# A decoder step on one core: 48 expert blocks multiplied in plain float32 instead of in split parts

## The chip, the core and the metric

The kernel runs on one core of a Trainium2 chip. The metric is the device time of one launch in microseconds. Times of the kernel before are from three runs; the trace is of one further execution, taken by the hardware profiler. The engines are TensorE (PE, and PEld for its weight loads), VectorE (DVE), ScalarE (ACT), GpSimd (POOL) and SyncE (SP, which here only issues transfers).

## What is computed

One inference step of a one-layer decoder over 512 prompt tokens and 64 sample tokens: a modulation by a condition vector, one combined projection, retention and dilated attention, an output projection and a layer norm, and then a layer of 16,384 experts with one row each in two tables:

```python
def block(xb):
    q = (xb @ w_q).reshape(PEER_BLOCK, H_PEER, 2, DK_PEER // 2)
    s = jnp.einsum('thsc,hskc->thsk', q, sub_keys).astype(jnp.float32)
    sv, si = lax.top_k(s, TOPK_PEER)
    cand = (sv[:, :, 0, :, None] + sv[:, :, 1, None, :]).reshape(PEER_BLOCK, H_PEER, TOPK_PEER * TOPK_PEER)
    cv, ci = lax.top_k(cand, TOPK_PEER)
    i0 = jnp.take_along_axis(si[:, :, 0], ci // TOPK_PEER, axis=-1)
    i1 = jnp.take_along_axis(si[:, :, 1], ci % TOPK_PEER, axis=-1)
    e = i0 * N_KEYS + i1
    g = jax.nn.softmax(cv, axis=-1)
    a = jax.nn.gelu(jnp.einsum('td,thkd->thk', xb, u_tab[e]), approximate=False)
    return jnp.einsum('thk,thkd->td', (g * a).astype(xb.dtype), v_tab[e])
```

D_MODEL is 1024, N_KEYS 128, H_PEER 8 and TOPK_PEER 16, so each token picks 128 experts. Everything is float32.

## The kernel before

The expert layer of the first 384 prompt tokens (three tiles of 128; ND = 384) is computed densely. The 16,384 experts are 128 blocks of 128. For block i the kernel multiplies the block's rows of u by the tokens' h2 (the input of the expert layer, transposed), takes the Gelu, multiplies by the block's gates and then by the block's rows of v, and adds up over the blocks in six PSUM banks. The remaining 128 prompt tokens and the 64 sample tokens take their experts by gathered rows: POOL issues the gathers (L1111), DVE multiplies (L1120, L1129), a few at each call of `advance`, which ties them to a point of the program by a copy of one element on POOL (`pace`, L1143).

A float32 product is made in **split parts**: `split` makes of x a rounded high part (ACT copy to the type fp32r) and the rest as a low part (a subtraction, to fp32r), and `mm3` (L423 to L425) does three matmuls, high by high, high by low and low by high. h2 lies split in the tiles `h2h` and `h2l`.

The program's order around the change:

- The w_q projection, the scores (L1458) and the selection of the 16 best (`top16`, DVE) for four tiles of tokens.
- `u_ahead(HEAD)`, with HEAD = 16: the u part of the first 16 of 48 blocks whose activations are computed ahead (those with i % 8 < 3). `u_part` loads the block (L1421, SP, 512 KB) into `wraw`, splits it (L1424 on ACT, L1425 on POOL), does 24 matmuls of 128x384 into a PSUM tile `tr` and the Gelu (L1430, ACT). `u_ahead` stores the result in DRAM (`actD`, L1439).
- `spread(t)` for three tiles: `route` (DVE, with one exponential on ACT, L1030) finds experts and gates; the **spread** then makes the gate of every token and expert. For four tokens at a time (a q; 32 q a tile, 96 in all) it builds one-hots: `oh1` on DVE (L1487), `oh0` one of four on ACT (L1493, L1494), one of four on POOL in every other q and the rest on DVE (L1496). Four plain float32 matmuls of 128x128 (L1497) multiply them, ACT copies the result to `stage` (L1498), and after eight q SP stores 2 MB in DRAM (L1502). After every fourth q one more ahead block is issued (`u_ahead(AHEAD)`), 24 in all.
- `u_ahead(128)` issues the last eight of the 48.
- The main loop over 128 blocks: gates are loaded for eight blocks at a time (L1578; 12 pieces, one for each store of the spread), the activation is loaded (L1589) or computed by `u_part`, and `v_part` loads v (L1558), splits it, multiplies activation and gates (`wt`, L1562) and does 18 matmuls of 128x512 for the block.

Instructions of one engine run in the order in which the scheduler laid them down, by a model of its own, when the program was built; engines wait for each other only where data or a buffer asks for it. The `wraw` tiles go round in 3 buffers (RB), the split parts in 4 (UB), the PSUM tiles `tr` in 2, the one-hots in 3.

Of the kernel before, what the change touches and what calls it, by code (L numbers as in the profile page):

```python
# [8 lines left out]
F32 = mybir.dt.float32  # L9
# [4 lines left out]
AF = mybir.ActivationFunctionType  # L14
OP = mybir.AluOpType
# [42 lines left out]
CU = 1  # L58
# [166 lines left out]
def body(tc, I, O, dbg=None):  # L225
    nc = tc.nc
    PE, DVE, ACT, POOL, SP = nc.tensor, nc.vector, nc.scalar, nc.gpsimd, nc.sync
# [6 lines left out]
    def fv(ap):  # L234
        return ap.bitcast(F32)

    def pool(name, side=None, space=None):
        kw = {"reuse_waits": "tile"} if space is None else {"space": space}
        if side:
            kw["side"] = side  # L240
        return tc.alloc_tile_pool(name=name, bufs=1, **kw)
# [17 lines left out]
    def tr_ps():  # L259
        return psum("tr", 2)  # L260
# [4 lines left out]
    def const(name, pl=P0, eng=SP):  # L265
        a = I[name]
        t = pl.tile(list(a.shape), F32, name="k" + name, tag="k" + name)
        eng.dma_start(t, a)
        return t
# [25 lines left out]
    def copy_old(n, ins):  # L295
        with tc.issue_after(ins):
            for _ in range(n):
                p = next(old, None)
                if p:
                    SP.dma_start(*p)  # L300
# [4 lines left out]
    def w_raw(pl=W, bufs=RB):  # L305
        return pl.tile([128, 1024], F32, name="wraw", tag="wraw", bufs=bufs)
# [126 lines left out]
    E = pool("halves", side="right")  # L433
# [21 lines left out]
    POOL.memset(cst, 0.0)  # L455
    SP.dma_start(cst[:, :, 0:9], I["cT"])
    ident = const("c_ident", eng=ACT)
    sel19 = const("c_sel", eng=ACT)
    iota = const("c_iota", eng=ACT)
    ACT.activation(cst[:, :, 0:9], cst[:, :, 0:9], AF.Silu)  # L460
    scT = A.tile([128, 8, 65], F32, name="scT")
# [56 lines left out]
    for g in range(NG):  # L518
        for o in range(VEC_G[g], VEC_G[g + 1], 512):
            e = min(o + 512, VEC_G[g + 1])  # L520
            ps = ac_ps()
# [529 lines left out]
    for c in range(2):  # L1051
        s = S1.tile([128, 4, 128], F32, name="scs", tag="scs", bufs=1)
        for z2 in range(2):
# [8 lines left out]
            ps = ac_ps()  # L1062
# [138 lines left out]
    for g in range(NG):  # L1201
# [8 lines left out]
        for hf in range(2):  # L1210
# [30 lines left out]
            for pp in range(2):  # L1241
# [38 lines left out]
                for c in range(4):  # L1280
                    for i, (vt, x, b) in enumerate(src[c]):
                        for h2, rows, hd, _ in heads:
                            PE.matmul(po[rows, 128 * c:128 * c + 128], v[vt][:, 64 * hd:64 * hd + 64], pts[h2][x][:, 128 * b:128 * b + 128],
                                      start=i == 0, stop=i == len(src[c]) - 1)
# [63 lines left out]
    ND = 128 * TD  # L1348
# [33 lines left out]
    h2h, h2l = [slot("x4"), slot("x5")], [slot("x6"), slot("x7")]  # L1382
    h2p = pair(h2h, h2l)
    ws = {}
    for c, ts in ((0, (0, 1, 2, 3)), (1, (0, 1, 2, 3)), (2, (0,)), (3, (0,)), (2, (1,)), (3, (1,)), (2, (2, 3)), (3, (2, 3))):
# [4 lines left out]
        for t in ts:  # L1390
            z = zs[t]
            ps = proj_n(w, mix, tiles[t])
# [23 lines left out]
    actD = {i: DR.tile([128, ND], F32, name=f"act{i}") for i in ahead}  # L1416
    ACTP = pool("act")

    def u_part(i):
        u = w_raw().rearrange("p (k e) -> p k e", e=128)  # L1420
        SP.dma_start(u, I["uT"][i])  # L1421
        uh = w_hi().rearrange("p (k e) -> p k e", e=128)
        ul = w_lo().rearrange("p (k e) -> p k e", e=128)
        ACT.activation(uh, u, AF.Copy)  # L1424
        POOL.tensor_tensor(ul, u, fv(uh), op=OP.subtract)  # L1425
        ps = tr_ps()
        for k in range(8):
            mm3(ps[:, 0:ND], (uh[:, k, :], ul[:, k, :]), h2p(k, slice(0, ND)), k == 0, k == 7)
        a = ACTP.tile([128, ND], F32, name="act", tag="act", bufs=4)
        ACT.activation(a, ps[:, 0:ND], AF.Gelu)  # L1430
        return a

    pre = iter(ahead)

    def u_ahead(n):
        for _ in range(n):
            i = next(pre, None)
            if i is not None:
                copy_old(CU, SP.dma_start(actD[i], u_part(i)).ins)  # L1439

    C = pool("route", side="right")
    sv = [C.tile([128, 16, 16], F32, name=f"sv{t}") for t in range(NT)]
    si = [C.tile([128, 16, 16], U32, name=f"si{t}") for t in range(NT)]
    C1 = pool("scores", side="right")
    for c in range(4):
        keys = C1.tile([128, 4, 128], F32, name="keys", tag="keys", bufs=2)
        SP.dma_start(keys, I["keysT"][:, 4 * c:4 * c + 4, :])
# [7 lines left out]
        for t in range(NT):  # L1455
            ps = ac_ps()
# [125 lines left out]
    for i in range(128):  # L1582
# [4 lines left out]
        if i in actD:  # L1587
            a = ACTP.tile([128, ND], F32, name="act", tag="act", bufs=4)
            SP.dma_start(a, actD[i])  # L1589
        else:  # L1590
            a = u_part(i)
# [41 lines left out]
```

## Time and profile before

| | us |
|---|---|
| three runs: median (lowest to highest) | 2486.14 (2481.27 to 2489.11) |
| the profiled execution: time, span | 2492.82, 2490.8 |
| busy in the span: PE, DVE, POOL, ACT | 2239.6, 1781.7, 1191.4, 1006.7 |

The mean granted clock of PE is 0.943 of full speed. All times within the profile count from the start of the span; the rows below are shown as the profile has them. A line such as "L1425 POOL TENSOR_TENSOR wlo<-wraw,whi 128x1024" names the line of the program, the engine, the operation and the tiles written and read. "Idle before" is the time in which that engine did nothing just before, with what released it. A float32 matmul is recorded as two pairs of a weight load and a pass. Matmuls overlap, so a single one's duration is longer than the step from one start to the next.

### The profile page before, as it was taken

The page shows a single profiled execution, that of the slowest core. Times are in us where ns is not written, and L with a number is a line of the kernel's source. Part 1 is how long each engine was busy: PE and PEld are TensorE (multiplying, and loading weights), DVE is VectorE, ACT ScalarE, POOL GpSimd, SP SyncE. Part 2 cuts the span into 40 slices and gives each one's busy share as a digit, 9 for nine tenths or more (in the row PEclk, how much of TensorE's full clock was granted, in tenths as well). Part 3 has the DMA queues.
Part 4 walks back from the last instruction along what each step waited for, and adds up shares of the span by engine and source line. Part 5 has one row for each costly group of instructions (what it writes and reads, how often), then busy time and mean ns, then how long its engine had stood idle before and what let it go on. Part 6 is the DMA issues. An engine that isn't in the chain of part 4 may idle for free.

```text
span 2490.8 us, 35646 instructions
## 1 busy us (share of the span) xinstructions
PE 2239.6 (90%) x12729; PEld 1894.2 (76%) x12729; DVE 1781.7 (72%) x3069; ACT 1006.7 (40%) x1661; POOL 1191.4 (48%) x942
## 2 busy tenths in 40 slices
PE   7889999958799996889888898799999999999995
PEld 4775566646777874889778888688888888888884
DVE  3463122255678778779999995888788888888875
ACT  2462222234455462233357786333333333333342
POOL 1021011043025645323566564877677777777742
PEclk7899999988899997899989999999999999999998
DMA  8786886566798997386767678799899999999951
GB/s 295 251 294 205 285 289 200 168 196 212 243 331 279 332 360 255 116 285 223 275 210 257 238 249 290 250 328 352 320 328 333 331 315 337 330 331 338 335 166 51
DMA packets 222494, 671.38 MB, mean 270 GB/s; under 512 B 27307, under 2 KB 80299, under 8 KB 218827
## 3 DMA queue, kind: packets, MB, share of 16 engines
q1 hardware_dynamic: 162016, 448.32, 52.6%
q0 software_dynamic: 59904, 220.62, 24.7%
q8 instruction: 100, 1.64, 0.3%
q14 instruction: 78, 0.64, 0.1%
q10 hardware_dynamic: 396, 0.16, 0.0%
HBM read 614.38 MB, written 112.40 MB: 292 GB/s over the span
## 4 chain that ended last, share of the span: by engine, by line
PE 51%; DVE 22%; DMA 12%; issue 6%; POOL 4%; ACT 3%; SPq 1%; POOLq 0%; DVEq 0%; ACTq 0%
PE mm L423 7%; PE mm L424 7%; PE mm L425 7%; PE tr L425 3%; PE tr L424 3%; PE tr L423 3%; DVE wlo L316 3%; PE ac L748 3%; DVE oh L1496 3%; DVE ys L1129 2%; PE ac L423 2%; PE ac L425 2%; PE ac L424 2%; DMA row<-in_u_dram,e 2%; POOL row L1111 1%
## 5 line engine op out<-in xcount | busy, mean ns | idle before, releaser
L316 DVE TENSOR_TENSOR wlo<-wraw,whi 128x1024 fp32r<-128x1024 f32 x304 | 415.3, 1370 | 266.7 <-ACT whi L315 243.0
L315 ACT ACTIVATE whi<-wraw 128x1024 fp32r<-128x1024 f32 x304 | 319.6, 1057 | 444.3 <-PE mm L424 171.5
L1425 POOL TENSOR_TENSOR wlo<-wraw,whi 128x1024 fp32r<-128x1024 f32 x128 | 336.1, 2626 | 134.1 <-ACT whi L1424 132.6
L423 PE MATMUL tr<-x,whi 128*128 128x384 f32 x1024 | 353.6, 345 | 23.6 <-ACT act L1430 13.1
L425 PE MATMUL tr<-x,wlo 128*128 128x384 f32 x1024 | 351.9, 344 | 7.3 <-POOL wlo L1425 7.2
L424 PE MATMUL tr<-x,whi 128*128 128x384 f32 x1024 | 351.2, 343 | 0.0
L1111 POOL DMA_INDIRECT row<-in_u_dram,e x192 | 261.9, 1364 | 138.3 <-DVE row L1120 97.6
L1111 POOL DMA_INDIRECT row<-in_v_dram,e x192 | 243.8, 1270 | 163.4 <-DVE y L1129 60.7
L423 PEld LDWEIGHTS tr<-x,whi 128*128 128x128 f32 x1024 | 197.4, 193 | 29.8 <-ACT act L1430 14.3
L1129 DVE SCALAR_TENSOR_TENSOR y<-row,acts,y 128x1024 f32<-128x1024 f32 x127 | 198.1, 1560 | 13.6 <-DMA row<-in_v_dram,e 12.9
L425 PEld LDWEIGHTS tr<-x,wlo 128*128 128x128 f32 x1024 | 196.5, 192 | 10.6 <-POOL wlo L1425 9.5
L424 PEld LDWEIGHTS tr<-x,whi 128*128 128x128 f32 x1024 | 197.1, 192 | 3.6
L1120 DVE SCALAR_TENSOR_TENSOR row<-row,h2g 128x1024 f32<-128x1024 f32 x128 | 177.8, 1408 | 15.0 <-DMA row<-in_u_dram,e 14.6
L1424 ACT ACTIVATE whi<-wraw 128x1024 fp32r<-128x1024 f32 x128 | 134.6, 1052 | 97.9 <-PE ac L425 38.1
L423 PE MATMUL mm<-xh,whi 128*128 128x512 f32 x384 | 155.1, 404 | 0.1
L424 PE MATMUL mm<-xl,whi 128*128 128x512 f32 x384 | 153.4, 400 | 0.0
L425 PE MATMUL mm<-xh,wlo 128*128 128x512 f32 x384 | 153.3, 399 | 0.0
L424 PE MATMUL ac<-wlo,wh 128*128 128x512 f32 x384 | 152.9, 398 | 0.0
L423 PE MATMUL ac<-whi,wh 128*128 128x512 f32 x384 | 152.2, 399 | 0.0
L315 ACT ACTIVATE wh<-wt 128x384 fp32r<-128x384 f32 x128 | 66.9, 524 | 206.1 <-DVE wt L1562 201.6
L425 PE MATMUL ac<-whi,wl 128*128 128x512 f32 x384 | 144.6, 394 | 0.0
L423 PE MATMUL mm<-whi,xh 128*128 128x256 f32 x448 | 133.5, 300 | 10.1 <-DVE gr L1359 5.6
(409 smaller groups left out, 5358.9 us busy)
## 6 DMA issues: line engine op xcount, KB each, us to landing
wraw<-in_uT_dram SPq DMA_DIRECT2D x128, 512.0 KB
wraw<-in_v_dram SPq DMA_DIRECT2D x128, 512.0 KB
out_dram<-in_cache_dram SPq DMA_DIRECT2D x64, 508.0 KB
wraw<-in_w_ada_dram SPq DMA_DIRECT2D x48, 512.0 KB
gate<-stage SPq DMA_DIRECT2D x12, 2048.0 KB
gt<-gate SPq DMA_DIRECT2D x192, 128.0 KB
kt<-in_kc_dram POOLq DMA_DIRECT2D x32, 588.0 KB
svt<-in_vc_dram SPq DMA_DIRECT2D x72, 256.0 KB
```

Source lines behind the costliest of these rows:

```text
L315: ACT.activation(hi, src, AF.Copy)
L316: return DVE.tensor_tensor(lo, src, fv(hi), op=OP.subtract).ins
L423: PE.matmul(ps, a[0], b[0], start=first, stop=False)
L424: PE.matmul(ps, a[0], b[1], start=False, stop=False)
L425: PE.matmul(ps, a[1], b[0], start=False, stop=last)
L748: PE.matmul(banks[bank][32 * p:32 * p + 32, a - 512 * bank:e - 512 * bank], qz[:, g, p, b2, :], kt[b2][:, a:e], start=b2 == 0, stop=b2 == 1)
L1111: POOL.indirect_dma_start(out=r, out_offset=None, in_=I[table], in_offset=bass.IndirectOffsetOnAxis(ap=e[:, j:j + 1], axis=0))
L1120: DVE.scalar_tensor_tensor(u, u, 1.0, h2, op0=OP.mult, op1=OP.mult, accum_out=a[:, j:j + 1])
L1129: DVE.scalar_tensor_tensor(y, v, a[:, j:j + 1], y, op0=OP.mult, op1=OP.add)
L1424: ACT.activation(uh, u, AF.Copy)
L1425: POOL.tensor_tensor(ul, u, fv(uh), op=OP.subtract)
L1496: (POOL if j < ON_ACT + ON_POOL[q % 2] else DVE).tensor_scalar(oh0[:, j, :], iota, col(0), col(2), op0=OP.is_equal, op1=OP.mult)
```

## The change

The 48 ahead blocks no longer go through `u_part` but through `u_plain`: eight plain float32 matmuls per block, of `wraw` as loaded and a new tile `h2f`, which holds h2 in float32 and is put together from `h2h` and `h2l` by two additions on DVE (L1457 after). The main loop's other 80 blocks keep `u_part`. A constant, `sel19`, moves to another pool, so that `h2f` finds room. Lines behind the insertion have numbers 14 higher (L1497 becomes L1511, L1502 L1516, L1578 L1592).

```diff
@@ -455,7 +455,7 @@
     POOL.memset(cst, 0.0)
     SP.dma_start(cst[:, :, 0:9], I["cT"])
     ident = const("c_ident", eng=ACT)
-    sel19 = const("c_sel", eng=ACT)
+    sel19 = const("c_sel", E, eng=ACT)
     iota = const("c_iota", eng=ACT)
     ACT.activation(cst[:, :, 0:9], cst[:, :, 0:9], AF.Silu)
     scT = A.tile([128, 8, 65], F32, name="scT")
@@ -1432,15 +1432,29 @@
 
     pre = iter(ahead)
 
+    def u_plain(i):
+
+        u = w_raw().rearrange("p (k e) -> p k e", e=128)
+        SP.dma_start(u, I["uT"][i])
+        ps = tr_ps()
+        for k in range(8):
+            PE.matmul(ps[:, 0:ND], u[:, k, :], h2f[:, k, :], start=k == 0, stop=k == 7)
+        a = ACTP.tile([128, ND], F32, name="act", tag="act", bufs=4)
+        ACT.activation(a, ps[:, 0:ND], AF.Gelu)
+        return a
+
     def u_ahead(n):
         for _ in range(n):
             i = next(pre, None)
             if i is not None:
-                copy_old(CU, SP.dma_start(actD[i], u_part(i)).ins)
+                copy_old(CU, SP.dma_start(actD[i], u_plain(i)).ins)
 
     C = pool("route", side="right")
     sv = [C.tile([128, 16, 16], F32, name=f"sv{t}") for t in range(NT)]
     si = [C.tile([128, 16, 16], U32, name=f"si{t}") for t in range(NT)]
+    h2f = C.tile([128, 8, ND], F32, name="h2f")
+    for kq in range(2):
+        DVE.tensor_tensor(h2f[:, 4 * kq:4 * kq + 4], fv(h2h[kq][:, :, 0:ND]), fv(h2l[kq][:, :, 0:ND]), op=OP.add)
     C1 = pool("scores", side="right")
     for c in range(4):
         keys = C1.tile([128, 4, 128], F32, name="keys", tag="keys", bufs=2)
```

The scheduler lays the instructions down anew. First place: PE from the last ahead matmuls in front of the spread to its first one-hot products (`ac<-oh`), before:

```order
L424 MATMUL tr<-x_8501,whi 128x384
L425 MATMUL tr<-x_8499,wlo 128x384
L423 MATMUL tr<-x_8499,whi 128x384
L424 MATMUL tr<-x_8501,whi 128x384
L425 MATMUL tr<-x_8499,wlo 128x384
L1497 MATMUL ac<-oh_11320,oh_11319 128x128
L423 MATMUL tr<-x_8499,whi 128x384
L1497 MATMUL ac<-oh_11334,oh_11333 128x128 x2
L1497 MATMUL ac<-oh_11320,oh_11319 128x128 x3
L1497 MATMUL ac<-oh_11334,oh_11333 128x128 x2
L1497 MATMUL ac<-oh_11348,oh_11347 128x128 x4
L424 MATMUL tr<-x_8501,whi 128x384
```

and with the change, where `tr<-h2f,wraw` are the plain matmuls:

```order
L1441 MATMUL tr<-h2f,wraw 128x384 x112
L1490 MATMUL tr<-kc_ident,i_10917 128x128 x2
L1490 MATMUL tr<-kc_ident,gw 128x128
L1441 MATMUL tr<-h2f,wraw 128x384 x13
L1511 MATMUL ac<-oh_11003,oh_11002 128x128 x4
L1511 MATMUL ac<-oh_11017,oh_11016 128x128 x4
L1511 MATMUL ac<-oh_11031,oh_11030 128x128 x4
L1441 MATMUL tr<-h2f,wraw 128x384 x10
L1511 MATMUL ac<-oh_11045,oh_11044 128x128 x4
L1511 MATMUL ac<-oh_11082,oh_11081 128x128 x4
L1511 MATMUL ac<-oh_11096,oh_11095 128x128 x4
L1441 MATMUL tr<-h2f,wraw 128x384 x9
```

Before, 414 split matmuls stand in front of the first one-hot product and 684 among the one-hot products, one to 24 at a time, with the one-hots of each q put in as they come. With the change 141 plain matmuls stand in front of it, and then 243 in portions of about ten behind every third q. On DVE the selection for the third tile (22 rows of `route` up to L998) stands in front of the first one-hots, where before only the second tile's did. On POOL the 48 subtractions of the ahead blocks are gone, and on ACT their 48 copies.

Second place: PE at the end of the spread, before:

```order
L1497 MATMUL ac<-oh_13699,oh_13698 128x128 x4
L423 MATMUL tr<-x_8499,whi 128x384
L424 MATMUL tr<-x_8501,whi 128x384
L425 MATMUL tr<-x_8499,wlo 128x384
L423 MATMUL tr<-x_8500,whi 128x384
L424 MATMUL tr<-x_8502,whi 128x384
L425 MATMUL tr<-x_8500,wlo 128x384
L423 MATMUL tr<-x_8500,whi 128x384
L424 MATMUL tr<-x_8502,whi 128x384
L425 MATMUL tr<-x_8500,wlo 128x384
L1497 MATMUL ac<-oh_13713,oh_13712 128x128 x4
```

and with the change (`mm<-whi,wh` is the first product of the main loop):

```order
L1511 MATMUL ac<-oh_12821,oh_12820 128x128 x4
L1511 MATMUL ac<-oh_12835,oh_12834 128x128 x4
L1511 MATMUL ac<-oh_12849,oh_12848 128x128 x4
L1511 MATMUL ac<-oh_12863,oh_12862 128x128 x4
L1511 MATMUL ac<-oh_12894,oh_12893 128x128 x4
L1511 MATMUL ac<-oh_12908,oh_12907 128x128 x4
L1511 MATMUL ac<-oh_12922,oh_12921 128x128
L1511 MATMUL ac<-oh_12936,oh_12935 128x128 x3
L1511 MATMUL ac<-oh_12922,oh_12921 128x128 x3
L1511 MATMUL ac<-oh_12936,oh_12935 128x128
L423 MATMUL mm<-whi,wh 128x512
L424 MATMUL mm<-wlo,wh 128x512
```

Before, 102 split matmuls of ahead blocks and of main-loop blocks 3 and 4 stand between the last one-hot product and the first product of the main loop. With the change nothing does: the last 21 q have no plain matmul among them, but the 48 split ones of blocks 3 and 4.

Third place: SP behind the last gate store (`gate<-stage`), before:

```order
L1502 DMA gate_10673<-stage 128x4096
L835 DMA l2b<-in_ln_b_dram 128x1024
L835 DMA l1ga<-in_ln_g_dram 128x1024
L835 DMA l1ba<-in_ln_b_dram 128x1024
L835 DMA gt2s<-modD 64x1x1024
L1439 DMA act_9165<-act 128x384
L1525 DMA x_14158<-xnD 64x1024
L1421 DMA wraw<-in_uT_dram 128x1024
L1525 DMA x_20743<-xnD 128x1024
L1439 DMA act_9166<-act 128x384
L1558 DMA wraw<-in_v_dram 128x1024
L1589 DMA act<-act_9120 128x384
```

and with the change:

```order
L1516 DMA gate_10676<-stage 128x4096
L835 DMA l2b<-in_ln_b_dram 128x1024
L835 DMA l1ga<-in_ln_g_dram 128x1024
L835 DMA l1ba<-in_ln_b_dram 128x1024
L1592 DMA gt<-gate_10672 128x256
L1592 DMA gt<-gate_10673 128x256
L1592 DMA gt<-gate_10674 128x256
L1592 DMA gt<-gate_10675 128x256
L835 DMA gt2s<-modD 64x1x1024
L1539 DMA x_13201<-xnD 64x1024
L1539 DMA x_19786<-xnD 128x1024
L1592 DMA gt<-gate_10676 128x256
```

The last row of the second piece is the piece of the first gate tile that waits for the store (`gt<-gate_10676`). Before, the corresponding row (`gt<-gate_10673`) is the one that follows the rows shown; it had an act store, loads of u and v and an act load in front of it which now stand ahead of the store, and four gate pieces now stand behind the store that stood ahead of it.

## Rows read from the trace of the kernel before

**Rows 1.** the chain of waits of the page, shares of the span by engine:

```profile
PE 51%; DVE 22%; DMA 12%; issue 6%; POOL 4%; ACT 3%; SPq 1%; POOLq 0%; DVEq 0%; ACTq 0%
```

**Rows 2.** windows, core 0: us, PE, PEld, DVE, ACT, POOL busy (instructions), PEclk, DMA share, GB/s:

```profile
1165.70:1528.40 362.70, 314.97 (x2005) 306.93 (x2004) 354.53 (x975) 238.75 (x410) 223.94 (x137) 0.95 0.69 242
...
1280.00:1464.00 184.00, 157.57 (x998) 151.74 (x999) 183.90 (x427) 139.86 (x245) 119.38 (x74) 0.94 0.67 236
1464.00:1528.00 64.00, 63.71 (x457) 63.55 (x457) 56.71 (x120) 61.01 (x108) 38.63 (x30) 1.00 0.74 265
1528.40:1560.50 32.10, 21.41 (x106) 20.59 (x105) 10.35 (x7) 10.69 (x13) 11.03 (x7) 0.79 0.97 321
...
1638.00:2400.00 762.00, 749.06 (x3606) 653.82 (x3605) 645.53 (x686) 268.77 (x359) 554.18 (x417) 1.00 0.91 323
```

**Rows 3.** timelines of PE, ACT, DVE: start, us, engine, line, operation [idle before <-releaser]:

```profile
1246.35 0.69 PE L423 MATMUL tr<-x,whi 128*128 128x384 f32 x1 [9.33 <-ACT act L1430]
...
1280.17 0.58 PE L1497 MATMUL ac<-oh,oh 128*128 128x128 f32 x1 [7.22 <-ACT oh L1494]
...
1243.24 0.31 ACT L1030 ACTIVATE cv<-ce 128x128 f32<-128x128 f32 x1 [11.89 <-DVE ce L1029]
...
1279.31 0.69 DVE L1487 TENSOR_TENSOR oh<-kc_iota,tT 128x512 f32<-128x512 f32 x1
```

**Rows 4.** timelines of DVE and of POOL, 1244 to 1263 us:

```profile
1246.64 2.47 DVE L1043 TENSOR_TENSOR gw<-cv,rsm 128x128 f32<-128x128 f32 x1
...
1251.42 1.21 DVE L1034 TENSOR_TENSOR eq<-eq,sif 128x2048 bf16<-128x2048 bf16 x1
...
1259.33 3.31 DVE L1034 TENSOR_TENSOR eq<-eq,sif 128x2048 bf16<-128x2048 bf16 x1
...
1244.57 6.78 POOL L1425 TENSOR_TENSOR wlo<-wraw,whi 128x1024 fp32r<-128x1024 f32 x2 [12.42 <-ACT whi L1424]
...
1258.81 2.75 POOL L1425 TENSOR_TENSOR wlo<-wraw,whi 128x1024 fp32r<-128x1024 f32 x1 [1.66 <-ACT whi L1424]
```

**Rows 5.** costliest groups of the page: POOL's subtraction; busy us, mean ns | idle before:

```profile
L1425 POOL TENSOR_TENSOR wlo<-wraw,whi 128x1024 fp32r<-128x1024 f32 x128 | 336.1, 2626 | 134.1 <-ACT whi L1424 132.6
```

**Rows 6.** timeline of PE, 1700 us: the first and last of eight split matmuls:

```profile
1700.22 0.33 PE L424 MATMUL tr<-x,whi 128*128 128x384 f32 x1
...
1701.44 0.34 PE L425 MATMUL tr<-x,wlo 128*128 128x384 f32 x1
```

**Rows 7.** timeline of PE: passes of plain matmuls, at 222 us and at 1466 us:

```profile
222.54 0.48 PE L748 MATMUL ac<-kt,qz 128*32 128x376 f32 x1
222.85 0.80 PE L748 MATMUL ac<-kt,qz 128*32 128x376 f32 x2
...
1466.05 2.04 PE L1497 MATMUL ac<-oh,oh 128*128 128x128 f32 x16
1467.84 0.42 PE L425 MATMUL tr<-x,wlo 128*128 128x384 f32 x1
```

**Rows 8.** groups by line from 1280 to 1530 us: the one-hot matmuls:

```profile
L1497 PE MATMUL ac<-oh,oh 128*128 128x128 f32 x768 | 111.3, 288 | 33.8 <-DVE oh L1496 14.1 <-DVE oh L1487 8.6 <-ACT oh L1494 8.2
```

**Rows 9.** timeline of ACT, 1284.9 to 1286.9 us, three kinds in a row:

```profile
1284.88 1.07 ACT L1498 ACTIVATE stage<-ac 128x512 f32<-128x512 f32 x1
1285.73 0.38 ACT L1493 ACTIVATE oh<-kc_iota,tT 128x128 f32<-128x128 f32 x1
1285.99 0.51 ACT L1494 ACTIVATE oh<-oh,tT 128x128 f32<-128x128 f32 x1
1286.37 1.12 ACT L1498 ACTIVATE stage<-ac 128x512 f32<-128x512 f32 x1
```

**Rows 10.** timelines of SP's issues and of PE, behind the last one-hot matmul:

```profile
1529.87 0.32 SPq L1502 DMA_DIRECT2D gate<-stage  x1
...
1547.86 0.33 SPq L1578 DMA_DIRECT2D gt<-gate  x1
...
1560.48 0.39 PE L423 MATMUL mm<-whi,wh 128*128 128x512 f32 x1
```

## The prediction, made before the changed kernel ran

> **What bounds the kernel now.** I read the chain of waits first, then the windows over the stretch that the diff touches, then that stretch's timelines engine by engine, and last the rows that give prices. The chain goes through TensorE for 51% of the span and through VectorE for 22% [rows 1]: TensorE bounds most of the program, and VectorE has a place of its own. The windows show where [rows 2]. From 1638 to 2400 us, the main loop, TensorE is busy for 749.06 of 762.00 us at full clock; nothing there is changed, so that stretch is carried over as it is. From 1165.7 to 1528.4 us, from the first matmul of an ahead block to the last one-hot matmul, TensorE is busy for 314.97 of 362.70 us at a mean clock of 0.95, while VectorE is busy for 354.53. In the piece from 1280 to 1464 us VectorE has 183.90 of 184.00: there it, not TensorE, sets the pace. From 1464 us both TensorE (63.71 of 64.00) and ScalarE (61.01) are full.
>
> Why VectorE is so slow there is in its rows beside POOL's [rows 4]. A multiply over 128x128 (L1043) took 2.47 us, and its end falls on the end of one of POOL's subtractions, whose two take 6.78 us from 1244.57; the 128x2048 multiply L1034 took 1.21 us with POOL idle and 3.31 us with the subtraction of 1258.81 beside it. So VectorE waits out POOL's subtraction, nearly one whole (mean 2.63 us) each time. I summed what VectorE's instructions from 1180 to 1550 us took over the time that the same lines take alone: about 80 us over some 46 subtractions (my estimate over all rows; these stand for it). TensorE's idle time hangs on it: it waits 9.33 us for a Gelu that stands in ScalarE's queue behind an exponential, which waited 11.89 us for VectorE, and 7.22 us for the first one-hot [rows 3]; in the spread it idles 33.8 us ahead of one-hot matmuls, most for VectorE [rows 8].
>
> The profiled execution took 2492.82 us, 6.68 above the median of 2486.14; I make the sum in its times and carry the difference over to the median.
>
> **What the change does, part by part.** Let T be the end of the last one-hot matmul, 1528.4 us.
>
> *TensorE, price of a block.* Removed: 24 split matmuls of 384 columns. Eight starts lie between 1700.22 and 1701.44, seven steps of 0.174 us [rows 6]: 24 x 0.1735 = 4.16 us. Added: 8 plain ones. No plain matmul of 128 weights by 384 columns is in the trace, so I bound it. A plain matmul is recorded as two passes. One pass of 376 columns shows 0.48 us alone and two together 0.80, so the second starts 0.32 us after the first [rows 7]; that is the lower bound (0.32 x 384 / 376 = 0.327 if all of it scales, less if the start of a pass is fixed). Sixteen passes of the one-hots take from 1466.05 to 1467.84 us, 0.112 each for 128 columns: three times that, 0.336, is the upper bound. I take 0.324, near the first, which has almost the size: 16 x 0.324 = 5.18 us a block, **+1.02 us**, and 48 x 1.02 = **+49 us** (bounds +46 and +58). Weight loads I cost at nothing: the one-hots load new weights for every 0.112 us pass and still keep that step, and here they have 0.324.
>
> The Trainium skill (FP8 and Floating Point Precision, TensorE Precision Notes) says that true FP32 takes four passes through the array. At four of the 0.1735 us steps a matmul would be 0.694 us and the 48 blocks +67 instead of +49; the trace shows two records of double length, which comes to 0.648, so the rows decide.
>
> *What lies before T.* The order of the change puts all 384 plain matmuls and 48 split ones of main-loop blocks 3 and 4 ahead of the last one-hot, where before 1098 split ones stood. At full clock TensorE's work from 1165.7 us to T was: 1098 x 0.1735 = 190.5, one-hots 768 passes x 0.1115 = 85.6, the rest of the w_q projection and scores 14, transposes 1: about 291. It becomes 384 x 0.648 = 248.8, 48 x 0.1735 = 8.3, and the same 85.6, 14 and 1: about 358, **+67 us** (49 of price, 18 of work that ran behind T). The stretch took 362.7 us, so 72 us of it were idle time and low clock (47.7 idle by the window; the rest is mostly matmuls at the lower level after waits).
>
> *How much of the 72 goes.* All 48 POOL subtractions go (48 x 2.63 = 126 us of POOL) [rows 5] and 48 copies of ScalarE; with them most of VectorE's 80 us. ScalarE's queue no longer holds a copy that the next block needs, so a late exponential does not stop the matmuls: these need only the load and a free PSUM bank. What I expect to stay:
> - The first one-hot. TensorE has 141 plain matmuls to do before it (1165.7 + 14 + 141 x 0.648 + 1 = 1272). VectorE began it at 1279.31 [rows 3]. It now has 24 us less of stretch before that (the part of the 80 up to there), but the new order puts the next tile's selection ahead of it, 22 us by its lines' own durations: about 1277.5. Wait 5 us (0 to 10).
> - The body. Groups of 3 q and 10 plain matmuls: 3 x 0.89 + 10 x 0.648 = 9.15 us of TensorE. VectorE's share of a group, by its lines' own durations, is 7.2 to 9.6 us in the first eight, which carry selection work, and under 4 after. Wait 1.5 us.
> - The tail. In the last 21 q no plain matmul is left. ScalarE needs 0.85 (stage copy) + 0.26 + 0.38 (one-hot) = 1.49 us per q [rows 9], and four copies for blocks 3 and 4: 35 us. TensorE has 21 x 0.89 + 8.3 = 27. ScalarE enters two q ahead at most: wait 8.5 us (3 to 12).
> - The two additions for h2f, 128x1536 on VectorE, lie where VectorE is half idle, at 1076 us: 1 us. The constant that changes pools costs nothing.
>
> Together 16 us of the 72 stay. So T moves by 67 - (72 - 16) = **+11 us**.
>
> *Behind T.* The first product of the main loop stands at 1560.48, 32.1 us after T, with DMA bound between: the last gate store is issued at 1529.87, the last piece of the first gate tile only at 1547.86 [rows 10]; transfers took 0.97 of this window at 321 GB/s [rows 2]. TensorE did 18 us of split matmuls meanwhile, which now have no place to hide; that is counted in the 67. In the new order the last act stores, the v loads and the act loads stand before the last gate store on SP, and only eleven transfers (some 4.5 MB with the store) stand between it and the last gate piece. At 321 GB/s that is 14 us for the 18; with less in the queue when it starts I take **-6 us** (bounds -13, as if only the 2 MB store and the pieces were waited for, and +3, for eight more small gate pieces behind it).
>
> Sum: +11 - 6 = **+5 us**: 2497.5 for the profiled execution, **2491** for the median.
>
> **The rivals.**
> 1. *Faster: VectorE's relief is worth all of the 72.* For it: with VectorE never behind, no wait row above is left but the first, and the queue behind T is shorter. Against: the ScalarE tail is arithmetic on rows. T would move by 67 - 66 = +1, and with -13 behind it the time is 12 less: 2474.
> 2. *Slower: VectorE still sets the pace in the first eight groups.* POOL keeps its one-hots and the gathers, and even where few subtractions were left VectorE's one-hots cost more than alone. The point that decides is a group of VectorE at more than TensorE's 9.15 us; the first eight stand at up to 9.6 without any stretch. At 1.5 us more in each, some 5 us more for the first one-hot and a few us of low clock after each of these waits, T is 17 to 20 us later: 2510. It is the one that makes the kernel slower with every price above right.
> 3. *Four passes at the step of a split matmul.* The same as the forecast with 18 us more: 2509. The two records per plain matmul speak against it. The Trainium skill's page named above would have it so.
>
> **How the numbers follow.** A measurement of this kernel tells about 0.3% from no change, 7.5 us, so faster is below 2478.7 and slower above 2493.6. The forecast (0.45) has its own range from 2482 to 2499, as the first one-hot, the tail and the boundary run to their ends together or against each other; two thirds of it are within 0.3%, one third slower. Rival 1 (0.23) is faster in nine cases of ten. Rival 2 (0.27) and rival 3 (0.05) are slower but for a sixth. Faster 0.21, same 0.36, slower 0.43. The range reaches to both rivals' places and the bound of the price (+58 where I took +49): 2470 to 2514.
>
> **What would show it.** Plain matmuls with passes 0.32 us apart, and 384 of them before T; no 128x128 instruction of VectorE near 2.5 us before 1460 us; the idle time before one-hot matmuls moved from VectorE to ScalarE and into the last 30 us before T; T near 1539; the first product some 26 us after it. Wrong it would be by a pass that is shorter or longer than 0.32 to 0.34 us, by a first one-hot later than 1285, or by a body in which TensorE waits for VectorE in each group; and if the main loop's stretch differs from 762 us by more than 3, work has moved that I did not see.

## The result

| | before | changed |
|---|---|---|
| median of nine runs each, us | 2489.11 (2476.11 to 2496.66) | 2500.93 (2493.24 to 2517.76) |
| profiled execution, us | 2492.82 | 2494.69 |

The ratio of the changed kernel to the kernel before is 1.0058, with a 95% interval from 1.0036 to 1.008: 9 to 20 us slower, some 14 by the middle. The time lies within the range given (2470 to 2514), which was drawn wide enough for the places of both rivals. The likeliest single case, +5 us and thus no difference that can be told, was not what came: the measured median lies 2 us above that case's own range (2482 to 2499).

The two profiled executions differ by 1.9 us only. The traces show where the rest lies: in the time up to the changed place. The rows below are, for either kernel, the last transposes of h2, up to which nothing is changed, and the one-hot matmuls; behind the colon stand the durations (least, median, most, ns), then the first and the last start. First the kernel before:

```profile
L1408 PE MATMUL tr<-kc_ident,h2g x8: 421/421/448, 1077.0 to 1078.5; 128*128 128x128 f32 x8
L1497 PE MATMUL ac<-oh,oh x768: 270/275/582, 1280.2 to 1528.4; 128*128 128x128 f32 x192
```

and the changed kernel:

```profile
L1408 PE MATMUL tr<-kc_ident,h2g x8: 418/418/445, 1064.2 to 1065.7; 128*128 128x128 f32 x8
L1511 PE MATMUL ac<-oh,oh x768: 272/275/580, 1263.9 to 1533.0; 128*128 128x128 f32 x192
```

The profiled execution of the kernel before came to the changed place 12.8 us later (1078.5 against 1065.7); over the twelve executions profiled in this study, one of each kernel, that point lies between 1065.7 and 1079.4 us. So I count from it. T, the start of the last one-hot matmul (the prediction calls 1528.4 its end), is 449.9 us behind it before and 467.3 in the changed kernel: **+17.4**. The end of the span is 1412.3 and 1427.2 us behind it: **+14.9**, close to the 14 of the runs.

The windows of the changed kernel that answer to [rows 2] (us, then busy time and instructions of PE, PEld, DVE, ACT and POOL, PEclk, DMA share, GB/s): up to the first one-hot, the spread, its last 21 q, the boundary, the main loop:

```profile
1167.00:1263.90 96.90, 94.69 (x298) 55.85 (x298) 95.10 (x438) 21.40 (x37) 7.23 (x8) 0.98 0.74 247
1263.90:1533.00 269.10, 257.08 (x1308) 188.72 (x1307) 172.57 (x471) 169.98 (x327) 94.07 (x87) 0.99 0.70 249
1491.00:1533.30 42.30, 32.56 (x218) 28.84 (x216) 30.57 (x70) 33.54 (x63) 24.22 (x24) 0.96 0.69 248
1533.00:1564.60 31.60, 0.46 (x3) 0.17 (x1) 12.67 (x17) 5.63 (x7) 7.39 (x4) 0.50 1.00 343
1638.00:2400.00 762.00, 746.78 (x3585) 652.54 (x3584) 641.75 (x680) 269.50 (x360) 553.40 (x415) 0.99 0.90 322
```

VectorE is no longer the bound: from 1263.9 to 1533 us it is busy for 172.57 of 269.10 us, where before it had 183.90 of 184.00 in the middle of the spread [rows 2]. TensorE has 257.08 of 269.10, at a clock of 0.99. The chain of waits of the page says the same; VectorE's share has gone from 22% [rows 1] to 10%:

```profile
PE 49%; DVE 10%; DMA 9%; issue 5%; POOL 3%; ACT 3%; SPq 0%; POOLq 0%; DVEq 0%; ACTq 0%
```

TensorE's timeline at the first one-hots (start, us, operation, idle time before) shows the new body:

```profile
1178.48 21.77 PE L1441 MATMUL tr<-h2f,wraw 128*128 128x384 f32 x67
...
1242.47 2.22 PE L1441 MATMUL tr<-h2f,wraw 128*128 128x384 f32 x4 [1.91 <-ACT act L1443]
...
1263.87 2.84 PE L1511 MATMUL ac<-oh,oh 128*128 128x128 f32 x24
...
1275.90 1.83 PE L1511 MATMUL ac<-oh,oh 128*128 128x128 f32 x14 [1.63 <-POOL oh L1510]
...
1283.38 2.84 PE L1511 MATMUL ac<-oh,oh 128*128 128x128 f32 x24
1286.06 6.62 PE L1441 MATMUL tr<-h2f,wraw 128*128 128x384 f32 x20
1292.51 2.84 PE L1511 MATMUL ac<-oh,oh 128*128 128x128 f32 x24
```

Sixty-seven passes of 384 columns take 21.77 us, the last of them 0.49 by itself: 21.28 / 66 = 0.322 us a pass. Twelve one-hot matmuls (24 passes) and ten plain ones (20 passes) alternate without a gap, 1283.38 to 1292.51, 9.13 us a group; the one wait of the early groups is 1.63 us, for POOL.

### The profile page after: what moved, and what is told of

It is laid out like the page before. It is cut to its first block, busy times and chain, and to the rows that moved or that the text cites. A ratio compares the mean times of both kernels' runs of the same rounds, so it can differ in the third digit from the quotient of the medians.

```text
span 2492.9 us, 34767 instructions
## 1 busy us (share of the span) xinstructions
PE 2268.0 (91%) x12345; PEld 1827.5 (73%) x12345; DVE 1710.4 (69%) x3071; ACT 955.6 (38%) x1613; POOL 1053.6 (42%) x894
## 4 chain that ended last, share of the span: by engine, by line
PE 49%; DVE 10%; DMA 9%; issue 5%; POOL 3%; ACT 3%; SPq 0%; POOLq 0%; DVEq 0%; ACTq 0%
PE tr L1441 8%; PE mm L423 6%; PE mm L424 6%; PE mm L425 6%; PE tr L425 3%; PE tr L424 3%; PE tr L423 3%; PE ac L1511 2%; PE ac L423 2%; PE ac L424 2%; PE ac L425 2%; DMA row<-in_u_dram,e 2%; POOL row L1111 2%; DVE wlo L316 2%; DMA row<-in_v_dram,e 1%
## 5 line engine op out<-in xcount | busy, mean ns | idle before, releaser
L315 ACT ACTIVATE whi<-wraw 128x1024 fp32r<-128x1024 f32 x304 | 319.4, 1056 | 445.1 <-PE mm L424 175.4
L1111 POOL DMA_INDIRECT row<-in_v_dram,e x192 | 244.1, 1271 | 175.9 <-DVE y L1129 53.4
L1111 POOL DMA_INDIRECT row<-in_u_dram,e x192 | 247.5, 1289 | 140.9 <-DVE row L1120 109.0
L1441 PE MATMUL tr<-h2f,wraw 128*128 128x384 f32 x768 | 254.6, 489 | 2.2 <-ACT act L1443 2.2
L1425 POOL TENSOR_TENSOR wlo<-wraw,whi 128x1024 fp32r<-128x1024 f32 x80 | 205.6, 2570 | 50.9 <-ACT whi L1424 48.8
L423 PE MATMUL tr<-x,whi 128*128 128x384 f32 x640 | 214.6, 335 | 2.8 <-ACT whi L1424 2.8
L1441 PEld LDWEIGHTS tr<-h2f,wraw 128*128 128x128 f32 x768 | 144.5, 191 | 97.7 <-ACT act L1443 3.1
L425 PE MATMUL tr<-x,wlo 128*128 128x384 f32 x640 | 215.3, 336 | 0.8 <-POOL wlo L1425 0.6
L424 PE MATMUL tr<-x,whi 128*128 128x384 f32 x640 | 214.9, 336 | 0.0
L1510 POOL TENSOR_SCALAR oh<-kc_iota,tT 128x128 f32<-128x128 f32 x48 | 64.9, 1352 | 206.0 <-PE ac L1511 136.3
L423 PE MATMUL mm<-whi,wh 128*128 128x512 f32 x256 | 103.4, 406 | 46.5 <-ACT wh L315 46.5
L1576 DVE TENSOR_TENSOR wt<-act,gt 128x384 f32<-128x384 f32 x128 | 93.3, 736 | 71.8 <-ACT act L1430 69.1
```

The lines of the kernel that those rows point to most:

```text
L315: ACT.activation(hi, src, AF.Copy)
L423: PE.matmul(ps, a[0], b[0], start=first, stop=False)
L424: PE.matmul(ps, a[0], b[1], start=False, stop=False)
L425: PE.matmul(ps, a[1], b[0], start=False, stop=last)
L1111: POOL.indirect_dma_start(out=r, out_offset=None, in_=I[table], in_offset=bass.IndirectOffsetOnAxis(ap=e[:, j:j + 1], axis=0))
L1441: PE.matmul(ps[:, 0:ND], u[:, k, :], h2f[:, k, :], start=k == 0, stop=k == 7)
```

## The experiments

All times are of runs beside runs of the kernel before on the same chip, whose medians were 2487 to 2491 us in these series; ratios are to these. The changed kernel was timed in the first series only, beside 2489.11, so its 2500.93 can be compared with a run's median to some 4 us.

**1. The subtraction on VectorE instead of POOL, nothing else.**

`low` is VectorE for the 48 ahead blocks and POOL for the others.

```diff
-        POOL.tensor_tensor(ul, u, fv(uh), op=OP.subtract)
+        low.tensor_tensor(ul, u, fv(uh), op=OP.subtract)
```

> The kernel before, split form kept, but the 48 subtractions of the ahead blocks run on VectorE instead of POOL. Theory A (VectorE's waiting behind POOL's subtractions, some 80 us, is what leaves TensorE idle): VectorE gets 48 x 1.15 = 55 us of work and loses the 80 us of waiting, TensorE pays no higher price; the last one-hot comes about 20 us earlier than 1528 and the time is 2465 to 2478. Theory B (the waits come from the order of the work and ScalarE's queue, and VectorE is simply full): VectorE has 55 us more to do in a stretch in which it is full, and the time is 2500 or more.

2462.19 us, ratio 0.9898 (0.9875 to 0.9921): 25 us faster than the kernel before and 39 faster than the changed one. T comes 429.0 us behind the transposes, 20.9 earlier than before. VectorE was given more work in the stretch in which it was the bound, and the stretch got shorter. Its rows in the spread of this run (groups by line: busy us, mean ns):

```profile
L1496 DVE TENSOR_SCALAR oh<-kc_iota,tT 128x128 f32<-128x128 f32 x233 | 69.1, 348 | 0.0
L1487 DVE TENSOR_TENSOR oh<-kc_iota,tT 128x512 f32<-128x512 f32 x93 | 63.4, 682 | 3.0 <-PE ac L1497 2.7
L1425 DVE TENSOR_TENSOR wlo<-wraw,whi 128x1024 fp32r<-128x1024 f32 x27 | 32.9, 1217 | 1.6 <-ACT whi L1424 1.5
```

Here 233 one-hots of 128x128 cost 348 ns each and 93 of 128x512 cost 682. In the kernel before the same two lines cost this, from 1280 to 1530 us:

```profile
L1496 DVE TENSOR_SCALAR oh<-kc_iota,tT 128x128 f32<-128x128 f32 x240 | 109.0, 503 | 0.0
L1487 DVE TENSOR_TENSOR oh<-kc_iota,tT 128x512 f32<-128x512 f32 x95 | 78.1, 822 | 4.7 <-PE ac L1497 4.7
```

503 and 822 ns, 45% and 21% more, with POOL's subtractions running. The two lines save 240 x 0.155 + 95 x 0.140 = 51 us; the 27 subtractions in this window cost VectorE 32.9. Theory B falls. The scheduler laid this run out in another order, though, on TensorE, VectorE and ScalarE: its 25 us are those of the subtraction's place and of that order together.

**2. The changed kernel, with an unused subtraction on POOL for every plain block.**

```diff
             PE.matmul(ps[:, 0:ND], u[:, k, :], h2f[:, k, :], start=k == 0, stop=k == 7)
+        ul = w_lo().rearrange("p (k e) -> p k e", e=128)
+        POOL.tensor_tensor(ul, u, h2f[:, :, 0:128], op=OP.subtract)
```

> The changed kernel, with one subtraction of 128x1024 on POOL added for each of the 48 plain blocks; its result is used by nothing. Theory A: VectorE's 128x128 instructions under such a subtraction take near 2.5 us again, the first one-hot comes 10 to 20 us later, TensorE waits for VectorE in the first eight groups; 10 to 30 us over the changed kernel, 2510 to 2530. Theory B (the spread is now TensorE's, whatever POOL does): within 5 us of the changed kernel's 2501.

2541.18 us, ratio 1.0209 (1.0186 to 1.0232): 40 us over the changed kernel, more than I expected, from work that nothing waits for but a buffer. VectorE and POOL in this run (timelines):

```profile
1298.42 3.22 DVE L1026 TENSOR_TENSOR cf<-cf 128x128 f32<-128x128 f32 x1
...
1297.50 1.68 POOL L1512 TENSOR_SCALAR oh<-kc_iota,tT 128x128 f32<-128x128 f32 x1
1299.16 2.34 POOL L1443 TENSOR_TENSOR wlo<-wraw,h2f 128x1024 fp32r<-128x1024 f32 x1
```

The same instruction in the kernel before, without a subtraction beside it:

```profile
1252.55 0.28 DVE L1026 TENSOR_TENSOR cf<-cf 128x128 f32<-128x128 f32 x1
```

The 128x128 instruction L1026 took 0.28 us there; here it takes 3.22, from 1298.42 to 1301.64, first beside a one-hot of POOL and then beside the subtraction, which runs from 1299.16 to 1301.50. TensorE's groups up to the first one-hot and ScalarE's row behind one of the waits:

```profile
L1441 PE MATMUL tr<-h2f,wraw 128*128 128x384 f32 x282 | 95.9, 502 | 12.7 <-ACT act L1445 12.7
L1513 PE MATMUL ac<-oh,oh 128*128 128x128 f32 x1 | 0.6, 550 | 2.6 <-DVE oh L1503 2.6
...
1229.28 0.31 ACT L1030 ACTIVATE cv<-ce 128x128 f32<-128x128 f32 x1 [13.28 <-DVE ce L1029]
```

TensorE waits 12.7 us for Gelus, which stand behind an exponential that waited 13.28 us for VectorE, and 2.6 us for the first one-hot. The first one-hot comes 215.6 us behind the transposes (198.2 in the changed kernel), the last 505.0 (467.3). In the spread VectorE's one-hots and TensorE's one-hot matmuls read:

```profile
L1512 DVE TENSOR_SCALAR oh<-kc_iota,tT 128x128 f32<-128x128 f32 x240 | 110.4, 509 | 0.0
...
L1513 PE MATMUL ac<-oh,oh 128*128 128x128 f32 x768 | 103.6, 290 | 20.4 <-DVE oh L1503 7.7 <-ACT oh L1510 5.8 <-DVE oh L1512 5.4
```

VectorE's one-hots are back at 509 ns (346 in the changed kernel), and TensorE waits 20.4 us ahead of one-hot matmuls (9.8 there), most of it for VectorE. Its plain matmuls in the spread wait for nothing, so it is not the `wraw` buffer, held longer, that costs. The order of the instructions is the changed kernel's, but for a few on TensorE. So the plain form does not make the spread TensorE's whatever POOL does; it makes it TensorE's because it takes POOL's work away.

**3 and 4. One half of the change at a time.** First plain for the first 16 blocks only, then for the 32 in the spread only:

```diff
-copy_old(CU, SP.dma_start(actD[i], u_plain(i)).ins)
+copy_old(CU, SP.dma_start(actD[i], (u_plain if i in ahead[:HEAD] else u_part)(i)).ins)
...
+copy_old(CU, SP.dma_start(actD[i], (u_part if i in ahead[:HEAD] else u_plain)(i)).ins)
```

> The changed kernel, but plain only for the first 16 ahead blocks; the 32 in the spread have the split form with POOL's subtraction again. Theory A: the stretch up to 1280 us gains what it does in the changed kernel (first one-hot 16 us earlier) for a price of 16 us of TensorE time that lies in its idle time, the body of the spread stays VectorE's as before, and the boundary behind the spread keeps split matmuls to do in its waiting: 2470 to 2482. Theory B (the price of plain matmuls is what costs, in proportion to the blocks): a third of the change's loss, 2493.

> The changed kernel, but the first 16 ahead blocks have the split form with POOL's subtraction; the 32 in the spread are plain. The complement of the run with the first 16 plain, which came to 2482. If the two halves of the change add up (the whole is +12 to +15, the first half -4), this is +16 to +19: 2503 to 2506. Theory A, which says that VectorE's waiting up to the first one-hot delays the whole spread and that the spread itself is bound by TensorE in the plain form, gives the same or more: 2503 to 2515. Theory B (the relief of VectorE in the spread is what the change gains): below the changed kernel, 2490 to 2500.

2482.47 us, ratio 0.9981 (0.9968 to 0.9995), for the first half; 2504.36 us, 1.0056 (1.0036 to 1.0075), for the second. The first half gains a little, just outside theory A's range; the second has the whole loss. The place of the first gain was not the expected one, though. The first one-hot came 201.3 us behind the transposes (201.7 before), because TensorE waited for VectorE:

```profile
L1511 PE MATMUL ac<-oh,oh 128*128 128x128 f32 x2 | 0.8, 486 | 5.4 <-DVE oh L1501 5.4
...
L1034 DVE TENSOR_TENSOR eq<-eq,sif 128x2048 bf16<-128x2048 bf16 x4 | 7.1, 1769 | 0.1
```

The new order puts the third tile's selection in front of the first one-hots, as in the whole change; TensorE has 2 us less to do there (128 plain and 35 split matmuls instead of 141 plain ones), and the first subtractions of the split blocks already hold VectorE up: its L1034 takes 1769 ns on the mean, 1220 in the changed kernel up to its first one-hot. What the first half gains lies behind T: T is 448.5 us behind the transposes (449.9 before), the end 958.5 us behind T (962.4 before). Why is open.

**5. The gathers of the main loop later.**

```diff
-    prev, gt_next, due, last = None, gates(0), 0.0, []
+    prev, gt_next, due, last = None, gates(0), -12.0, []
...
-        advance(int(due), a, steps)
-        due -= int(due)
+        advance(max(int(due), 0), a, steps)
+        due -= max(int(due), 0)
```

> The changed kernel, but the main loop's gathers of expert rows start about four blocks later and then run at the same rate. Theory A (the 31 us between the last one-hot and the first product of the main loop are DMA bound, and the 4 MB of gathers in them, which the kernel before did not have there, keep the gate pieces waiting): 8 to 12 us shorter than the changed kernel, 2489 to 2493. Theory B (the last gate store and the constants' loads ahead of the pieces set it): no difference, 2499 to 2503.

2504.0 us, ratio 1.0059 (1.0036 to 1.0081): no gain that the runs show. The boundary itself did get shorter, 25.4 us against 31.6 in the changed kernel. Its software queue, that of the gathers, and what that queue moved in the same window of the kernel before and of the changed kernel:

```profile
q0 software_dynamic: 83, 0.34, 3.7%
```

```profile
q0 software_dynamic: 656, 2.36, 18.7%
```

0.34 MB before, 2.36 MB in the changed kernel, none in this run. So the gathers do lengthen the boundary by some 6 us. T is 3.2 us earlier as well (464.1 us behind the transposes): no gather stands in front of POOL's last one-hot any more. From the first product to the end the run needs 931.0 us instead of 928.3. Counted from the transposes, its profiled execution is 6.7 us shorter than that of the changed kernel (1420.5 us against 1427.2), near what theory A said; the medians, of six runs that spread over 12 us and of nine that spread over 25, show none of it. Whether the gathers cost anything in the whole stays open.

**6. No one-hots on ScalarE.**

```diff
-ON_ACT = 1
+ON_ACT = 0
```

> The changed kernel, but ScalarE builds no one-hots: all four of each q are VectorE's, or POOL's one in every other q. The scheduler then spreads the plain blocks up to the last q and leaves 24 plain and 24 split matmuls (20 us) behind it. Theory A (the loss of the change lies in the last 21 q, where ScalarE with its 1.5 us per q holds TensorE up by some 13 us, and behind them in 31 us in which TensorE has nothing to do): the last one-hot comes 25 to 33 us earlier, the 20 us hide behind it, and the time is 2468 to 2480. Theory B (TensorE's 49 us of price are the loss, wherever the matmuls stand; VectorE gets 25 us more one-hots): 2495 to 2510.

2481.19 us, ratio 0.9955 (0.9935 to 0.9975): 20 us under the changed kernel and some 10 under the kernel before, with every plain matmul still paid. T comes 431.3 us behind the transposes, 36 earlier than in the changed kernel. TensorE's one-hot matmuls in this run and in the changed kernel (from 1271 to 1505 and from 1263 to 1534 us; idle time before them and for whom):

```profile
L1511 PE MATMUL ac<-oh,oh 128*128 128x128 f32 x768 | 96.6, 276 | 3.5 <-POOL oh L1510 1.8 <-DVE oh L1510 1.2 <-ACT stage L1512 0.2
```

```profile
L1511 PE MATMUL ac<-oh,oh 128*128 128x128 f32 x768 | 95.4, 279 | 9.8 <-ACT oh L1508 5.8 <-POOL oh L1510 2.6 <-DVE oh L1510 0.7
```

The waits for ScalarE are gone, and the gain is more than they were: 24 plain and 24 split matmuls, 20 us, now run behind T. The boundary takes 34.6 us, 3 more than in the changed kernel, with TensorE busy for 22.26 of them. Not all of the 36 us stay won: from the first product to the end this run needs 940.3 us against 928.3, of which 4 are the 24 split matmuls of block 4, which now stand behind the first product; the rest I did not trace.

**7. The last three plain blocks held behind the spread, with ScalarE's one-hots.** It separates the two halves of run 6.

```diff
-    u_ahead(128)
+    u_ahead(5)
+    with tc.issue_after(lastoh.ins):
+        u_ahead(128)
```

> The changed kernel, ScalarE's one-hots kept, but the last three plain blocks are held back until the last one-hot matmul is issued, so that 24 plain and 24 split matmuls stand behind it, as in the run without one-hots on ScalarE (2481). It separates the two halves of that run's gain. Counted from the last transposes of h2, the last one-hot came at 467 us in the changed kernel and at 431 there. Theory A (20 us of the 36 come from the matmuls that hide behind the spread, the rest from ScalarE's tail): ScalarE's 1.5 us per q now holds for 26 q without plain blocks, the last one-hot comes at 445 to 450, the time is 2482 to 2490. Theory B (ScalarE's tail was the smaller part, below 5 us): 431 to 438 and 2476 to 2482.

2492.99 us, ratio 1.0012 (0.9995 to 1.0029). T lies 443.9 us behind the transposes: 23 us of run 6's 36 come with the matmuls behind T, 13 with ScalarE's one-hots. T is a little earlier than theory A gave, and the time 3 us later: the boundary takes 36.3 us, and from the first product to the end are 937.4. The tail (TensorE, then ScalarE):

```profile
1489.64 1.16 PE L1511 MATMUL ac<-oh,oh 128*128 128x128 f32 x8 [0.65 <-ACT oh L1508]
1491.43 2.05 PE L1511 MATMUL ac<-oh,oh 128*128 128x128 f32 x16 [0.63 <-ACT oh L1508]
1494.14 1.16 PE L1511 MATMUL ac<-oh,oh 128*128 128x128 f32 x8 [0.65 <-ACT oh L1508]
...
1489.77 1.06 ACT L1512 ACTIVATE stage<-ac 128x512 f32<-128x512 f32 x1
1490.62 0.38 ACT L1507 ACTIVATE oh<-kc_iota,tT 128x128 f32<-128x128 f32 x1
1490.88 0.88 ACT L1508 ACTIVATE oh<-oh,tT 128x128 f32<-128x128 f32 x2
1491.65 1.07 ACT L1512 ACTIVATE stage<-ac 128x512 f32<-128x512 f32 x1
1492.51 0.38 ACT L1507 ACTIVATE oh<-kc_iota,tT 128x128 f32<-128x128 f32 x1
1492.77 1.05 ACT L1512 ACTIVATE stage<-ac 128x512 f32<-128x512 f32 x1
1493.61 0.47 ACT L1508 ACTIVATE oh<-oh,tT 128x128 f32<-128x128 f32 x1
```

Three q take 4.5 us (1489.64 to 1494.14), 1.5 us a q, with ScalarE at work without a gap; TensorE's own work for three q is 2.68 us. This is the price per q that the prediction took from [rows 9].

**8 to 10. Versions that might beat run 1.** Plain for the 9th to 16th ahead block and for all of the first 16, with VectorE's subtraction for the others; and run 1 with one one-hot on POOL in every q.

```diff
+copy_old(CU, SP.dma_start(actD[i], u_plain(i) if i in ahead[8:HEAD] else u_part(i, DVE)).ins)
...
+copy_old(CU, SP.dma_start(actD[i], u_plain(i) if i in ahead[:HEAD] else u_part(i, DVE)).ins)
...
-ON_POOL = (1, 0)
+ON_POOL = (1, 1)
```

> Split form with VectorE's subtraction for 40 ahead blocks, plain for the 9th to the 16th. In the run with all 48 on VectorE (2462) TensorE waits 15 us for VectorE before the first one-hot and loses 4 more at the low clock. Eight plain blocks take 9 us off VectorE there and put 8 us on TensorE where it waits. Theory A: the first one-hot 6 to 9 us earlier, 2452 to 2458. Theory B (the price of plain matmuls comes out in full, or the scheduler's new order gives it away): 2462 to 2470.

> As the run before this one, with all of the first 16 ahead blocks plain. TensorE is then without a wait up to the first one-hot and pays 16 us there for 19 us of waiting, and the order puts all split matmuls but four in front of the last one-hot, so that the boundary hides 11 us less. Theory A: 2460 to 2470, no better than with none plain. Theory B (less work on VectorE is better whatever TensorE pays): below 2455.

> The kernel before with the ahead blocks' subtraction on VectorE (2462), and one of four one-hots of every q on POOL instead of every other q: 48 x 0.26 = 12 us less on VectorE, and POOL has room since the subtractions are gone. Theory A (what is left of TensorE's waits in the spread, some 11 us, is for VectorE): 2454 to 2459. Theory B (POOL's one-hots, 1.1 to 1.35 us each, come late or hold VectorE up in their turn): 2462 or more.

2459.46 us (ratio 0.9861, 0.9835 to 0.9887), 2466.24 (0.9903, 0.9877 to 0.9928) and 2466.06 (0.9901, 0.9873 to 0.9929). The three intervals overlap with run 1's. Eight plain blocks may gain a few us, between the two theories; sixteen gain nothing, as theory A had it; more one-hots on POOL gain nothing, as theory B had it. These runs fit the reading that, with the subtraction off POOL, plain blocks are worth at most what TensorE waits for VectorE at the place where they stand; they do not prove it.

## Why the prediction was right, and where it was off

*VectorE waits for POOL, and TensorE for VectorE: shown.* Run 2 puts POOL's subtractions back in the order of the changed kernel, and the time follows by +40 us; run 1 takes them away in the split form, in an order of its own, and it follows by -25. The Trainium skill (SBUF — State Buffer, Who interferes with whom) says that a VectorE instruction with two inputs in SBUF contends with a GpSimd instruction that reads SBUF. That agrees with the 0.28 us that become 3.22 in run 2. It calls the ports that the two share an exclusive lock; the VectorE row that ends 0.14 us behind the subtraction agrees with it.

*The price of a block: right.* 16 passes of 0.322 us are 5.16 us against 4.16, +48 us for 48 blocks; I had +49. No time for weight loads shows on top of that. Rival 3's price, four steps of a split matmul, would have been 0.694 us a matmul and +67; the trace has two recorded passes of 0.322, so it is out. The four passes through the array that the Trainium skill (FP8 and Floating Point Precision, TensorE Precision Notes) gives for true FP32 are not refuted by that: whether a recorded pass is one of them or two, no run here shows.

*The body: right.* No group waits for VectorE, and one waits 1.63 us for POOL. Rival 2 named a T later by 17 to 20 us, which is what came (+17.4), but its mechanism, VectorE at over 9.15 us a group, did not act: the early groups stand 9.13 us apart. Rival 1 had T later by 1 us; the tail and the boundary, below, kept it from that.

*Up to the first one-hot: the time right, its parts not.* It came at 198.2 us behind the transposes, and 1277.5 in the prediction is 199. But the 5 us of waiting for VectorE that I had put there did not come: no idle time stands before the row at 1263.87. TensorE was late by itself, with 2.2 us of waits for Gelus and passes at a lower clock behind them (granted 0.87 from 1237 to 1250 us). That the sum still fits is luck. I had said that a late exponential no longer stops the matmuls. It still does, by the Gelu that empties the PSUM bank: 1.91 us in the changed kernel, 12.7 us in run 2.

*The tail: the step that was mis-sized, first part.* The wait was put at 8.5 us, from ScalarE's 35 us against TensorE's 27. From 1491.4 us to the end of the last one-hot at 1533.3 are 41.9 us, so it was 15: TensorE was idle for 9.7 of 42.30 us in that window, and the rest of the 15 are passes that took longer, single ones behind a wait or at a lower clock. ScalarE was busy for 33.54 of the 42.30 us, so it waited too. Here are TensorE's rows at the end, one of ScalarE's and three of POOL's:

```profile
1514.30 2.84 PE L1511 MATMUL ac<-oh,oh 128*128 128x128 f32 x24
...
1523.64 1.16 PE L1511 MATMUL ac<-oh,oh 128*128 128x128 f32 x8 [1.45 <-ACT oh L1508]
1525.14 2.05 PE L1511 MATMUL ac<-oh,oh 128*128 128x128 f32 x16 [0.34 <-ACT oh L1508]
1527.85 0.49 PE L1511 MATMUL ac<-oh,oh 128*128 128x128 f32 x2 [0.66 <-DVE oh L1510]
1529.32 1.11 PE L1511 MATMUL ac<-oh,oh 128*128 128x128 f32 x6 [0.98 <-ACT oh L1508]
1531.38 2.08 PE L1511 MATMUL ac<-oh,oh 128*128 128x128 f32 x8 [0.95 <-POOL oh L1510]
...
1515.39 1.10 ACT L1512 ACTIVATE stage<-ac 128x512 f32<-128x512 f32 x1 [1.94 <-PE ac L1511]
...
1528.37 0.96 POOL L1111 DMA_INDIRECT row<-in_u_dram,e  x1 [0.16 <-issue]
1529.34 0.18 POOL L1143 COPY pace<-act 1x1 f32<-1x1 f32 x1
1529.51 1.82 POOL L1510 TENSOR_SCALAR oh<-kc_iota,tT 128x128 f32<-128x128 f32 x1
```

The order puts 19 or 20 split matmuls at once between two q; ScalarE has nothing to copy meanwhile (1.94 us idle at 1515.39) and is late for the next q when they are done. The last one-hot of POOL stands behind a gather and a copy of the main loop's on POOL's queue, and the last q waits for it (0.95 us, then eight passes at a granted clock of 0.50, the lower of the two levels, 2.08 us). Run 5, without the gather, has T 3.2 us earlier. I had taken the larger of two engines' sums; two engines that wait for each other in turn need more than either. Runs 6 and 7 differ by 13 us of T, which is what ScalarE's one-hots cost there.

*Behind T: the second part.* I gave -6 us, because fewer transfers stand ahead of the last gate piece. The boundary took 31.6 us after 32.1. SP's rows for the last gate store and the last gate piece:

```profile
1535.01 0.32 SPq L1516 DMA_DIRECT2D gate<-stage  x1
...
1555.34 8.14 SPq L1592 DMA_DIRECT2D gt<-gate  x13
```

From the one to the other are 20.3 us, where before there were 18.0 and I had worked out 14. The eleven transfers have 5.4 MB by their sizes, not the 4.5 that I wrote, so 16.7 us at 321 GB/s. And they were counted on SP's queue only; POOL was ahead with the gathers and put 2.36 MB into the same window. That is not because it had lost its subtractions: run 2, which has them back, has 2.63 MB of gathers there, and run 1, which lacks them, 0.45. It comes with the new order, in which the activations that `pace` waits for are ready before T: the first of these copies starts at 1523.95 us, before it was at 1554.04. Run 5, without the gathers, has 16.7 us between the two rows (1537.79 to 1554.44) and a boundary of 25.4 us, as I expected, but its runs show no shorter time.

*The sum.* +11 and -6 gave +5 (on 2492.8 that is 2497.8, not the 2497.5 written there; and the shares of the cases add up to 0.38 for no change and 0.42 for slower, not 0.36 and 0.43). With 15 in place of 8.5 in the tail and -0.5 in place of -6 it is +17, and +14.9 was seen between the transposes and the end; from the first product on the changed kernel needs 2 us less, 928.3 after 930.3, which is not explained. Both errors went the same way and carried the result over the 0.3% that divides no change from slower. The direction of each step was right; the two sizes that were worked out for engines and queues one at a time were off.

*Where the expected gain went.* TensorE does lose nearly all its idle time up to 1491 us: 4.5 us are left of 47.7. It pays for it with 48 us of slower matmuls and with 18 us of matmuls that ran behind T for nothing before; 31 us behind T are idle now (TensorE busy for 0.46 of 31.60). Run 7 puts three blocks back there and is 8 us faster than the changed kernel.

## What to carry to other kernels

Where two engines share something, price the instruction on each of them together with what it does to the other: a subtraction of 1.2 us on the engine that is the bound was cheaper than one of 2.6 us on a less busy engine beside it. Before a slower form of an operation is bought to get rid of a helper's work, try the helper's work elsewhere. And a wait that is bound by transfers is a place for matmuls: an order that empties it to do the work earlier has to count that work on the path.

## What was not expected

- A POOL subtraction that nobody reads cost 40 us for 48 of them, 0.83 us each, in a kernel in which VectorE had a third of its time free in the spread.
- Without POOL's subtractions VectorE's 128x128 one-hots cost 348 ns on the mean, with them 503; ScalarE's one-hot rows hardly change (L1494 493 ns and 492).
- Up to the changed place the twelve profiled executions need from 1065.7 to 1079.4 us, a spread of 13.7 us, about as much as the effect of the change. Two single profiles can be compared only from a common point.
